# A third block of 128 output channels in the input-projection stage: the first LRU gate block accumulated while the modulation weights stream in

## The chip, the cores and the metric

The kernel runs on one core of one Trainium2 chip. The metric is the device time of one launch in microseconds; the kernel before takes 1186.78 us (median of three runs, 1185.78 to 1189.39). Matmuls run on TensorE (PE in the profile, its weight loads are PEld), elementwise work on VectorE (DVE), ScalarE (ACT) and GpSimd (POOL); SyncE (SP) issues most of the DMAs.

## The reference, cut to what matters

The block is one transformer layer on 1024 tokens of width 1024. What the change touches is its first third:

```python
mod = jnp.dot(jax.nn.silu(c), w_mod[l]) + b_mod[l]           # 1024 x 6144
shift1, scale1, gate1, shift2, scale2, gate2 = jnp.split(mod[:, None, :], 6, axis=-1)
h = rms_norm(x, g_norm1[l]) * (1.0 + scale1) + shift1
proj = jnp.dot(h, w_in[l])                                   # 1024 x 2560
x_lru, z_lru, q, k, v = jnp.split(proj, SPLITS, axis=-1)     # 512 channels each
...
y_lru = (h_fwd + h_bwd) * jax.nn.gelu(z_lru)
```

`x_lru` goes through a short convolution and two gated linear recurrences (the LRU); `z_lru` gates the result. Attention on q, k, v, an output projection and a mixture of 16 experts follow; the experts fill the time from about 615 us to the end.

## The kernel before, in words

Every float32 operand of a matmul is split in two float32r parts, high and low (`split`, L140: ACT copies the high part, another engine subtracts it to get the low part). A product is three matmuls: high by high, high by low, low by high. A block of 128 output channels over 1024 tokens and 1024 inputs (8 input tiles k = 0 to 7) takes 8 x 3 x 2 = 48 matmuls with 512 columns.

**The first stage** (L378 to L441) makes h and at once multiplies it with the first 256 columns of `w_in` (x_lru's channels 0 to 255, two blocks of 128, accumulated in the PSUM tiles `px[0]` and `px[1]`, named pjx). It goes input tile by input tile, since each tile of h needs its own 128 columns of shift and of scale, that is 1 MB of `w_mod`. The steps for one k are:

- `m_load(k)` (L282): four 256 KB DMAs on SP, `w_mod` into the tiles wm.
- `m_mm(k)` (L294): PE multiplies wm by silu(c) into the PSUM tile mp, for all 8 row blocks where k < 4 and for 4 of them (RP) where k >= 4.
- `m_sum(k)` (L301): DVE copies mp into acc; for k >= 4 it does the other 4 row blocks itself, four SCALAR_TENSOR_TENSOR of line L311, the first of which reads mp from PSUM and the other three only SBUF.
- `m_red(k)` (L315): four small matmuls of acc with ones, into pm: the sum over partitions.
- `m_col(k)` (L320): two small DVE operations make the column of 1 + scale and of shift.
- `h_make(k)` (L326): ACT makes the high part `hh`; ACT (k = 3 to 6) or DVE makes h in float32; POOL (k = 7: DVE) subtracts to get the low part `hl`, line L336.
- `x_mm(k, lo)` (L341): eight matmuls of pjx with hh (lo False) or four with hl (lo True).

In this stage PE, DVE and ACT run in the order in which the lines stand (`manual_schedule`, L378). For loop step k (L413 to L441) that is: `m_mm(k+2)`, `m_sum(k+2)`, the hh part of `x_mm(k)`, the hl part of `x_mm(k-1)`, `m_red(k+2)`, `m_col(k+2)`, `h_make(k+2)`. The weights' other half is split at step 1 (ACT) and step 3 (DVE, `w0_split(1,1)`), the small `lam_table` stands at step 4. SP and POOL are ordered by a scheduler, except that each DMA of the stage is tied behind the one before it (`issue_after(lds[-1])`).

**After it**, PE computes q and k (`proj_qk`, token tiles against 256 channels), the LRU of block 0 (`do_lru(0)`), more q and k, `do_lru(1)`, then the gate blocks z 0 and z 1 (`do_z`, L637: `proj_ch`, 48 matmuls into pjz; then `fin_lru`, Gelu on ACT and a product on DVE), with `mod_out(0)` (mq) between them, then the second half of x_lru, v, and so on. `mod_rest` (L619) adds up the remaining four sixths of the modulation on DVE (macc, L624) from 512 KB DMAs (wr). Weights come in 512 KB halves through five raw slots and six split slots (NRA, NSP). PSUM has two slots of tag pg and two of tag pj; px holds one of each during the first stage, pm used the other pg and mp the other pj.

Of the kernel before, what the change touches and what calls it, by code (L numbers as in the profile page):

```python
# [8 lines left out]
F32 = mybir.dt.float32  # L9
F32R = mybir.dt.float32r  # L10
# [3 lines left out]
ALU = mybir.AluOpType  # L14
# [48 lines left out]
KV = (7,)  # L63
KH = (0, 1, 2, 7)
KB = (0, 1, 2, 7)
CAP = 128
RPAD = 56
EPS = 1e-6
# [14 lines left out]
def tile_block(ctx: ExitStack, tc, x, cols, w_mod, b_mod, w_in, wa, wx, lam_qk, relT, w_out, g2, w_router,  # L83
# [8 lines left out]
    def mm(out, lhsT, rhs, start, stop):  # L92
        return T.matmul(out, lhsT=lhsT, rhs=rhs, start=start, stop=stop)  # L93
# [40 lines left out]
    def raw_tile(name, shape):  # L134
        return rawA.tile(shape, F32, tag="raw", bufs=NRA, name=name)
# [4 lines left out]
    def split(src, hi, lo, eng=None):  # L140
        act(hi, src)
        return (eng or V).tensor_tensor(out=lo, in0=src, in1=hi.bitcast(F32), op=ALU.subtract)  # L142

    def load_half(c0, kk, eng):
        r = raw_tile(f"wi{c0}_{kk}", [P, 4, 256])
        SY.dma_start(out=r, in_=w_in[kk * 512:(kk + 1) * 512, c0:c0 + 256].rearrange("(k p) c -> p k c", p=P))
        hi = strm.tile([P, 4, 256], F32R, tag="s", bufs=NSP, name=f"wi{c0}_{kk}h")
        lo = strm.tile([P, 4, 256], F32R, tag="s", bufs=NSP, name=f"wi{c0}_{kk}l")
        split(r, hi, lo, eng)
        return hi, lo  # L150

    def load_in(c0, eng):
        return [load_half(c0, kk, eng) for kk in range(2)]

    phb = ExitStack()
    psb = phb.enter_context(tc.tile_pool(name="psb", bufs=1, space=PSUM, reuse_waits="tile"))
# [125 lines left out]
    def m_load(k):  # L282
        for rh in range(2):
            w = raw_tile(f"wm{k}_{rh}", [P, 4, 2, P]) if rh else v_tile(f"wm{k}_{rh}", [P, 4, 2, P])
            for g in range(2):
                c0 = g * 1024 + k * P
                with tc.issue_after(lds[-1].ins):
                    lds.append(SY.dma_start(out=w[:, :, g, :],
                                            in_=w_mod[rh * 512:(rh + 1) * 512, c0:c0 + P].rearrange("(r p) c -> p r c", p=P)))
            wm[k, rh] = w  # L290
# [2 lines left out]

    def m_mm(k):  # L294
        if RP[k]:
            mps[k] = psb.tile([P, 2, P], F32, tag="pj", bufs=2, name=f"mp{k}")
        for r in range(RP[k]):
            g = 32 * (r % 4)
            mm(mps[k][g:g + 32], scz[:, r, :], wm[k, r // 4][:, r % 4], r < 4, r + 4 >= RP[k])
# [13 lines left out]
            V.tensor_tensor(out=part[0], in0=part[0], in1=part[1], op=ALU.add)  # L313

    def m_red(k):  # L315
        pms[k] = psb.tile([P, 2], F32, tag="pg", bufs=2, name=f"pm{k}")
        for g in range(2):
            mm(pms[k][:, g:g + 1], accs[k][:, g, :], ones32[:, 0:1], True, True)

    def m_col(k):  # L320
        pm = pms[k]
        V.scalar_tensor_tensor(out=acol[:, k:k + 1], in0=pm[:, 1:2], scalar=bs1[:, k:k + 1], in1=col[:, C_G1 + k:C_G1 + k + 1],
                               op0=ALU.add, op1=ALU.mult)
        V.tensor_tensor(out=shc[:, k:k + 1], in0=pm[:, 0:1], in1=col[:, C_BM + k:C_BM + k + 1], op=ALU.add)
# [16 lines left out]
    def x_mm(k, lo, ms=(0, 1)):  # L341
        for m in ms:
            wh, wl = (w[:, k % 4, m * P:(m + 1) * P] for w in ws0[k // 4])
            for lt, h_ in ((wh, hl[k]),) if lo else ((wh, hh[k]), (wl, hh[k])):
                for n in range(2):
                    mm(px[m][:, n * 512:(n + 1) * 512], lt, h_[:, n * 512:(n + 1) * 512],
                       k == 0 and lt is wh and not lo, k == KT - 1 and lo)

    w0r, wq0 = [], []

    def w0_load(kk):
# [18 lines left out]
    w0_load(0)  # L370
    for k in range(1, 4):
        m_load(k)
        if k == KM:
            w0_load(1)
    with tc.issue_after(lds[-1].ins):
# [2 lines left out]
    with tc.manual_schedule(engines={mybir.EngineType.PE, mybir.EngineType.DVE, mybir.EngineType.Activation}):  # L378
        c_silu()
        tables_a()  # L380
        act(rst[:, 0:1], epsc, AF.Sqrt)
        for t in range(NT + 1):
            if t < NT:
                x_stat(t)
            if 1 <= t <= NT:
                if t == NT:
                    m_mm(0)
                    m_sum(0)
                x_flip(t - 1)
                if t == NT:  # L390
                    m_red(0)
            if 2 <= t <= NT:
                x_evac(t - 2)
        w0_split(0, 0)
        m_col(0)
        x_evac(NT - 1, (0,))
        m_mm(1)
        warm(WU1)
        w0_split(0, 1)
        m_sum(1)  # L400
        h_make(0)
        m_red(1)
        m_col(1)
        x_evac(NT - 1, (1,))
        h_make(1)
        x_mm(0, False)
        m_mm(2)
        m_sum(2)
        x_mm(1, False, (0,))
        m_red(2)  # L410
        m_col(2)
        h_make(2)
        for k in range(1, KT + 1):  # L413
            if k + 3 < KT:
                m_load(k + 3)
            if k + 2 < KT:
                m_mm(k + 2)
                m_sum(k + 2)
            if k == KS:
                w0_split(1, 1)  # L420
            if k == 1:
                x_mm(0, True)
            if k == KLT:
                lam_table()
            if k < KT:
                x_mm(k, False, (0, 1) if k > 1 else (1,))
            if 1 < k < KT:
                x_mm(k - 1, True)
            if k + 2 < KT:
                m_red(k + 2)  # L430
                m_col(k + 2)
                i_act, i_pv = h_make(k + 2)
                if k + 2 < KT - 1:
                    i_pool = i_pv
                else:
                    i_dve = i_pv
            if k == KS0:
                w0_split(1, 0)
            if k + 2 in (KW, KW + 1):
                wq0.append(load_half(1024, k + 2 - KW, V))  # L440
        x_mm(KT - 1, True)  # L441
    sm1_.close()


# [51 lines left out]
    def do_lru(ct):  # L496
        xc = xc_[ct]
        xh = lt_(f"xch{ct}", None, F32R)
        xl = lt_(f"xcl{ct}", None, F32R)
        split(xc, xh, xl, V if ct in LV else G_)  # L500
        hs, st = [], []
        for d in range(2):
            pre = []
            for gi in range(2):
                pg = psb.tile([P, 1024], F32, tag="pg", bufs=2, name=f"pg{ct}_{d}_{gi}")
                i = d * 4 + ct
                for wi_, (w_, xv) in enumerate(((bdh, xh), (bdl, xh), (bdh, xl))):
                    for n in range(2):
                        mm(pg[:, n * 512:(n + 1) * 512], w_[gi][:, i, :], xv[:, n * 512:(n + 1) * 512], wi_ == 0, wi_ == 2)
                tg = lt_(f"tg{ct}_{d}_{gi}")  # L510
                act(tg, pg, AF.Tanh, scale=0.5, bias=hb[:, gi * 8 + i:gi * 8 + i + 1])
                pre.append(tg)
            ta, ti = pre
            i = d * 4 + ct
            tt = lt_(f"tt{ct}_{d}")
            act(tt, ta, AF.Tanh, scale=nkap[:, i:i + 1], bias=nkap[:, i:i + 1])
            act(ta, ta, AF.Exp, scale=kap[:, i:i + 1], bias=kap[:, i:i + 1])
            sq = lt_(f"sqa{ct}_{d}")
            act(sq, ta, AF.Square)
            V.scalar_tensor_tensor(out=tt, in0=sq, scalar=1.0, in1=tt, op0=ALU.add, op1=ALU.mult)  # L520
            V.scalar_tensor_tensor(out=ti, in0=ti, scalar=1.0, in1=xc, op0=ALU.add, op1=ALU.mult)
            st.append((ta, ti, tt))
        for d in range(2):
            ta, ti, tt = st[d]
            act(tt, tt, AF.Sqrt, scale=0.25)
            G_.tensor_tensor(out=ti, in0=ti, in1=tt, op=ALU.mult)
            if d == 0:
                V.tensor_tensor_scan(out=tt, data0=ta, data1=ti, initial=0.0, op0=ALU.mult, op1=ALU.add)
            else:
                V.tensor_tensor_scan(out=tt[:, ::-1], data0=ta[:, ::-1], data1=ti[:, ::-1], initial=0.0,  # L530
                                     op0=ALU.mult, op1=ALU.add)
            hs.append(tt)
        V.tensor_tensor(out=hs[0], in0=hs[0], in1=hs[1], op=ALU.add)
        hs_[ct] = hs[0]

    def fin_lru(ct, ps):
        ge = lt_(f"ge{ct}")
# [99 lines left out]
    def do_z(ws, cp, m):  # L637
        fin_lru(2 * cp + m, proj_ch(ws, m, f"pjz{cp}_{m}"))
# [3 lines left out]
    with tc.issue_after(conv.ins):  # L642
        mod_rest(0, 0, 1)
    do_lru(0)
    wq1 = load_in(1280, G_)
    mod_rest(0, 2)
    proj_qk(wk0, 1, 0)
# [3 lines left out]
    proj_qk(wq1, 0, 1)  # L651
    do_lru(1)
    mod_rest(0, 5)
    wz0 = load_in(512, G_)
    proj_qk(wk1, 1, 1)
    mod_rest(0, 6, 7)
    wx1 = load_in(256, V)
    do_z(wz0, 0, 0)
    pend.pop()[1]()
    mod_out(0)  # L660
    mod_new(1)
    do_z(wz0, 0, 1)
    mod_rest(1, 0, 1)
    wr = lru.tile([P, KT, NE], F32, name="wr")
    A.dma_start(out=wr, in_=w_router.rearrange("(k p) e -> p k e", p=P))
# [796 lines left out]
```

## Time and profile before

| | |
|---|---|
| median of 3 runs | 1186.78 us (1185.78 to 1189.39) |
| the profiled execution | 1189.59 us, its span 1187.8 us |
| PE / PEld busy | 94% / 79% of the span |
| DVE / ACT / POOL busy | 80% / 67% / 41% |
| mean granted TensorE clock | 0.979 |

The times of instructions are microseconds from the span's start. A busy share is an average over stages; how a stage is bound is read in its own stretch. An idle time in brackets stands at the instruction that ended it, with what released it.

### The profile page before, as it was taken

Reading aid. Unit: us, or ns where it says so; the run is one execution under the profiler, and the core shown is the slowest. Engines: PE = TensorE matmul, PEld = TensorE weight load, DVE = VectorE, ACT = ScalarE, POOL = GpSimd, SP = SyncE. Lnnn points to the kernel's source line nnn. Section 1 sums busy time; section 2 is a strip of 40 time slices with the busy share of each in tenths; the row PEclk is TensorE's granted clock in tenths of the full one; section 3 lists DMA queues with packets and bytes.
Section 4 is the critical chain, followed back from the end, with each engine's and each line's share of the span. In section 5 each row is a group of like instructions: output and inputs, shape, how many; then the busy total and the mean of one; then the engine's idle time right before and its main releaser. Section 6 shows DMA issues by size and latency. Waiting matters only on the chain.

```text
span 1187.8 us, 17864 instructions
## 1 busy us (share of the span) xinstructions
PE 1115.3 (94%) x6319; PEld 935.9 (79%) x6320; DVE 955.2 (80%) x1241; ACT 791.6 (67%) x1046; POOL 484.1 (41%) x540
## 2 busy tenths in 40 slices
PE   6999899999699999999649999999999999999996
PEld 4699898888588899777538788888888888888885
DVE  6797657874298897444579999999999999999995
ACT  7548282394177788544318788878887888888784
POOL 4693232133087547243544334443324444322400
PEclk9899999999899999999969999999999999999999
DMA  9765725723844604534799999999999999999911
GB/s 334 225 195 171 238 72 186 241 71 63 203 108 117 176 6 143 186 113 163 263 337 345 358 377 385 392 408 393 375 394 393 367 397 406 394 394 387 392 46 18
DMA packets 147889, 303.82 MB, mean 256 GB/s; under 512 B 17996, under 2 KB 44748, under 8 KB 147796
## 3 DMA queue, kind: packets, MB, share of 16 engines
q1 hardware_dynamic: 134864, 279.46, 65.9%
q0 software_dynamic: 5488, 19.45, 6.4%
q10 hardware_dynamic: 7448, 3.77, 1.1%
q8 instruction: 50, 0.82, 0.3%
q14 instruction: 39, 0.32, 0.1%
HBM read 277.42 MB, written 25.22 MB: 255 GB/s over the span
## 4 chain that ended last, share of the span: by engine, by line
PE 73%; DVE 7%; DMA 6%; POOL 6%; issue 5%; ACT 2%; SPq 0%; POOLq 0%; ACTq 0%; DVEq 0%
PE ab L93 28%; PE y L93 13%; PE mix L93 7%; PE pjk L93 3%; PE pjz L93 3%; PE pv L93 3%; PE sc L93 3%; POOL wo L886 2%; PE pjv L93 2%; DMA wr<-in_w_mod_dram 2%; PE pw L814 1%; PE pjx L93 1%; PE pf L1346 1%; PE pg L93 1%; DVE macc L624 1%
## 5 line engine op out<-in xcount | busy, mean ns | idle before, releaser
L1246 POOL TENSOR_SCALAR oh<-iot,slot 128x128 bf16<-128x128 bf16 x120 | 146.3, 1234 | 252.2 <-PE pf L1346 252.2
L93 PE MATMUL ab<-wh,xeh 128*128 128x512 f32 x512 | 202.0, 395 | 0.2 <-ACT xeh L90 0.2
L93 PE MATMUL ab<-wh,xel 128*128 128x512 f32 x512 | 199.7, 390 | 0.1
L93 PE MATMUL ab<-wl,xeh 128*128 128x512 f32 x512 | 157.7, 389 | 0.0
L93 PEld LDWEIGHTS ab<-wl,xeh 128*128 128x128 f32 x512 | 96.1, 188 | 20.3
L93 PEld LDWEIGHTS ab<-wh,xel 128*128 128x128 f32 x512 | 96.2, 188 | 19.4 <-DVE xel L1259 0.5
L93 PEld LDWEIGHTS ab<-wh,xeh 128*128 128x128 f32 x512 | 96.1, 188 | 19.4 <-ACT xeh L90 0.5
L142 DVE TENSOR_TENSOR wl<-w_0r,wh 128x1024 fp32r<-128x1024 f32 x79 | 96.8, 1226 | 10.2 <-ACT wh L90 0.4
L90 ACT ACTIVATE wh<-w_0r 128x1024 fp32r<-128x1024 f32 x81 | 86.0, 1062 | 24.9 <-PE ab L93 14.9
L142 DVE TENSOR_TENSOR wl<-w_3r,wh 128x1024 fp32r<-128x1024 f32 x79 | 96.6, 1224 | 6.2
L90 ACT ACTIVATE wh<-w_1r 128x1024 fp32r<-128x1024 f32 x79 | 83.5, 1058 | 23.6 <-PE ab L93 18.9
L90 ACT ACTIVATE wh<-w_3r 128x1024 fp32r<-128x1024 f32 x79 | 83.9, 1062 | 21.9 <-PE ab L93 18.2
L142 DVE TENSOR_TENSOR wl<-w_2r,wh 128x1024 fp32r<-128x1024 f32 x80 | 96.3, 1220 | 2.4 <-ACT wh L90 0.5
L90 ACT ACTIVATE wh<-w_2r 128x1024 fp32r<-128x1024 f32 x80 | 84.7, 1060 | 18.9 <-PE ab L93 17.9
L142 DVE TENSOR_TENSOR wl<-w_1r,wh 128x1024 fp32r<-128x1024 f32 x78 | 92.6, 1220 | 3.8 <-ACT wh L90 2.1
L768 DVE CUSTOM_DVE_ANT_0 p<-sc,bias 128x1024 f32<-128x1024 f32 x64 | 77.7, 1214 | 18.0 <-PE sc L93 18.0
L93 PE MATMUL y<-wh,htl 128*128 128x512 f32 x256 | 82.9, 395 | 0.0
L93 PE MATMUL y<-wh,hth 128*128 128x512 f32 x256 | 80.9, 396 | 0.0
L93 PE MATMUL y<-wl,hth 128*128 128x512 f32 x256 | 79.6, 391 | 0.0
L90 ACT ACTIVATE p<-p,stat 128x1024 f32<-128x1024 f32 x62 | 70.8, 1151 | 4.8 <-DVE stat L768 4.8
L93 PEld LDWEIGHTS pv<-v,wt 128*128 128x128 f32 x512 | 61.7, 192 | 2.4
L93 PE MATMUL pv<-v,wt 128*128 128x128 f32 x512 | 62.1, 275 | 0.0
(458 smaller groups left out, 2858.5 us busy)
## 6 DMA issues: line engine op xcount, KB each, us to landing
w_0r<-in_w_dram SPq DMA_DIRECT2D x81, 512.0 KB, 8.5
w_1r<-in_w_dram SPq DMA_DIRECT2D x79, 512.0 KB, 8.8
w_2r<-in_w_dram SPq DMA_DIRECT2D x78, 512.0 KB, 9.0
w_3r<-in_w_dram SPq DMA_DIRECT2D x77, 512.0 KB, 8.7
wr<-in_w_mod_dram SPq DMA_DIRECT2D x32, 512.0 KB, 4.7
wi<-in_w_in_dram SPq DMA_DIRECT2D x18, 512.0 KB, 4.7
w_5r<-in_w_dram SPq DMA_DIRECT2D x17, 512.0 KB, 6.8
wm<-in_w_mod_dram SPq DMA_DIRECT2D x32, 256.0 KB, 4.9
```

The lines of the kernel that those rows point to most:

```text
L90: return A.activation(out=out, in_=in_, func=func, **kw)
L93: return T.matmul(out, lhsT=lhsT, rhs=rhs, start=start, stop=stop)
L142: return (eng or V).tensor_tensor(out=lo, in0=src, in1=hi.bitcast(F32), op=ALU.subtract)
L624: V.scalar_tensor_tensor(out=macc[i], in0=w, scalar=sc[:, k:k + 1], in1=macc[i], op0=ALU.mult, op1=ALU.add)
L768: V.tensor_tensor_reduce(out=p_, in0=scp[g, j], in1=prs[h][0][:, b0:b0 + S], op0=ALU.add, op1=ALU.min, scale=1.0, scalar=3.0e38, accum_out ...
L814: T.transpose(pw[:, b * P:(b + 1) * P], pt_[g, 0][:, kt * P:(kt + 1) * P], ident)
L886: G_.tensor_tensor(out=r[:, qs], in0=r[:, qs], in1=gate1[:, qs], op=ALU.mult)
L1246: G_.tensor_scalar(out=oh[:, t, :], in0=iot, scalar1=slot[:, e, t:t + 1], scalar2=None, op0=ALU.is_equal)
L1346: T.transpose(pt[:, b * P:(b + 1) * P], sa[:, b * P:(b + 1) * P], ident)
```

## The change

z's first block (columns 512 to 639 of `w_in`) is moved into the first stage as a third block beside the two of x_lru. Its weights are one 512 KB DMA, issued between the modulation weights of k = 2 and of k = 3, into tiles of their own; they are split at step 1, the high part on ACT, the low part on DVE. `z_mm(k)` is six matmuls into the PSUM tile pz0, at the end of step k+1's PE work. In each step `m_red(k+2)` and `m_col(k+2)` now stand ahead of the hl part of `x_mm(k-1)`. Since pz0 takes the pg slot that pm used, pm for k > 2 lives in the second bank of mp's tile. The Gelu of z block 0 follows the stage at once, its product follows `do_lru(0)`. z's second block is loaded as one 512 KB column tile later on and stands alone where both stood.

```diff
+    def split_col(r, hi, lo, eng):
+        split(r, hi, lo, eng)
+        return [(hi[:, 4 * kk:4 * kk + 4, :], lo[:, 4 * kk:4 * kk + 4, :]) for kk in range(2)]
+
+    def load_col(c0, eng):
+        r = raw_tile(f"wc{c0}", [P, KT, P])
+        SY.dma_start(out=r, in_=w_in[:, c0:c0 + P].rearrange("(k p) c -> p k c", p=P))
...
     def m_mm(k):
         if RP[k]:
-            mps[k] = psb.tile([P, 2, P], F32, tag="pj", bufs=2, name=f"mp{k}")
+            mps[k] = psb.tile([P, 8, P], F32, tag="pj", bufs=2, name=f"mp{k}")[:, 0:5]
+            if k > 2:
+                pms[k] = mps[k].rearrange("p a b -> p (a b)")[:, 512:514]
+            mps[k] = mps[k][:, 0:2]
...
+    wz = [sm1.tile([P, KT, P], F32 if c == "r" else F32R, name=f"wz{c}") for c in "rhl"]
...
+    def z_load():
+        with tc.issue_after(lds[-1].ins):
+            lds.append(SY.dma_start(out=wz[0], in_=w_in[:, CZ:CZ + P].rearrange("(k p) c -> p k c", p=P)))
+
+    def z_split():
+        wzs[:] = split_col(*wz, V)
+
+    def z_mm(k):
+        if not pz:
+            pz.append(psb.tile([P, 1024], F32, tag="pg", bufs=2, name="pz0"))
+        wh, wl = (w[:, k % 4, :] for w in wzs[k // 4])
+        for lt, h_ in ((wh, hh[k]), (wh, hl[k]), (wl, hh[k])):
+            for n in range(2):
+                mm(pz[0][:, n * 512:(n + 1) * 512], lt, h_[:, n * 512:(n + 1) * 512], k == 0 and lt is wh and h_ is hh[k],
+                   k == KT - 1 and lt is wl)
...
     for k in range(1, 4):
         m_load(k)
+        if k == 2:
+            z_load()
...
                 x_mm(k, False, (0, 1) if k > 1 else (1,))
-            if 1 < k < KT:
-                x_mm(k - 1, True)
             if k + 2 < KT:
                 m_red(k + 2)
                 m_col(k + 2)
+            if 1 < k < KT:
+                x_mm(k - 1, True)
+            if k == KS0:
+                z_split()
+            if k < KT:
+                z_mm(k - 1)
+            if k + 2 < KT:
                 i_act, i_pv = h_make(k + 2)
...
         x_mm(KT - 1, True)
+        z_mm(KT - 1)
+        ge0 = ylp.tile([P, S], F32, tag="y", bufs=NCT, name="ylru0")
+        act(ge0, pz[0], AF.Gelu_apprx_tanh)
...
+    def fin_first():
+        V.tensor_tensor(out=ge0, in0=hs_[0], in1=ge0, op=ALU.mult)
+        y_lru.append(ge0)
...
     do_lru(0)
+    fin_first()
...
-    wz0 = load_in(512, G_)
+    wz0 = load_col(CZ + P, G_)
     proj_qk(wk1, 1, 1)
     mod_rest(0, 6, 7)
     wx1 = load_in(256, V)
-    do_z(wz0, 0, 0)
+    fin_lru(1, proj_ch(wz0, 0, "pjz0_1"))
     pend.pop()[1]()
     mod_out(0)
     mod_new(1)
-    do_z(wz0, 0, 1)
```

## Rows read from the trace of the kernel before

**Rows 1.** Stretches: length; PE, PEld, DVE, ACT, POOL busy; granted clock; DMA share; GB/s.

```profile
33.50:39.00 5.50, 2.89 (x12) 2.05 (x12) 5.37 (x4) 3.17 (x3) 4.55 (x2) 0.98 1.13 338
39.00:46.00 7.00, 6.95 (x25) 5.09 (x26) 5.04 (x7) 2.48 (x2) 2.41 (x1) 0.53 0.82 256
46.00:60.50 14.50, 14.50 (x81) 11.55 (x80) 11.19 (x23) 10.45 (x10) 10.17 (x13) 1.00 0.49 126
62.00:175.90 113.90, 108.45 (x855) 105.24 (x854) 83.50 (x64) 69.15 (x68) 50.07 (x39) 1.00 0.53 171
```

**Rows 2.** PE in order of time: start, us, instruction, idle before it and its releaser.

```profile
32.81 0.64 PE L93 MATMUL mp<-wm,scz 128*32 128x256 f32 x8
...
39.05 1.02 PE L93 MATMUL pm<-ones,acc 128*128 128x1 f32 x4 [2.66 <-DVE acc L311]
...
46.00 0.50 PE L93 MATMUL pm<-ones,acc 128*128 128x1 f32 x4
46.43 0.64 PE L93 MATMUL mp<-wm,scz 128*32 128x256 f32 x8
47.00 0.73 PE L93 MATMUL pjx<-hh,w0h 128*128 128x512 f32 x2
...
49.86 0.50 PE L93 MATMUL pm<-ones,acc 128*128 128x1 f32 x4
...
53.72 0.50 PE L93 MATMUL pm<-ones,acc 128*128 128x1 f32 x4
...
60.55 0.28 PE L93 MATMUL pjq<-wi_0h,hh 128*128 128x256 f32 x1
```

**Rows 3.** POOL in order of time, the same columns.

```profile
30.13 0.85 POOL L377 TENSOR_TENSOR lp<-lq 128x128 f32<-128x128 f32 x1 [2.46 <-DMA lq<-in_lam_qk_dram]
30.95 4.75 POOL L336 TENSOR_TENSOR hl<-h,hh 128x1024 fp32r<-128x1024 f32 x2
35.84 2.35 POOL L336 TENSOR_TENSOR hl<-xT,hh 128x1024 fp32r<-128x1024 f32 x1
43.02 2.41 POOL L336 TENSOR_TENSOR hl<-xT,hh 128x1024 fp32r<-128x1024 f32 x1 [4.83 <-ACT xT L90]
49.45 2.38 POOL L336 TENSOR_TENSOR hl<-xT,hh 128x1024 fp32r<-128x1024 f32 x1 [4.03 <-ACT xT L90]
```

**Rows 4.** The chain that ended last, pieces on DVE from 33.5 to 39 us.

```profile
33.52 0.49 DVE acc L311
...
34.03 1.96 DVE acc L311
...
36.02 2.46 DVE acc L311
...
38.51 0.50 DVE acc L311
```

**Rows 5.** DVE in order of time, the same columns as PE's.

```profile
43.10 3.40 DVE L363 TENSOR_TENSOR w0l<-w,w0h 128x1024 fp32r<-128x1024 f32 x1
46.54 0.22 DVE L322 SCALAR_TENSOR_TENSOR acol<-pm,bs,col 128x1 f32<-128x1 f32 x1
...
47.13 0.48 DVE L311 SCALAR_TENSOR_TENSOR acc<-wm,sc,mp 128x256 f32<-128x256 f32 x1 [0.32 <-PE mp L93]
47.65 1.53 DVE L311 SCALAR_TENSOR_TENSOR acc<-wm,sc,acc 128x256 f32<-128x256 f32 x3
...
57.60 1.22 DVE L142 TENSOR_TENSOR wi_0l<-wi,wi_0h 128x1024 fp32r<-128x1024 f32 x1
```

**Rows 6.** The chain that ended last, from 170 to 200 us.

```profile
175.94 10.91 PE pjz L93 x48
```

**Rows 7.** ACT in order of time, the same columns.

```profile
33.24 1.25 ACT L90 ACTIVATE hh<-xT,shc,acol 128x1024 fp32r<-128x1024 f32 x1 [2.15 <-DVE shc L324]
...
68.91 1.06 ACT L90 ACTIVATE bdh<-bd 128x1024 fp32r<-128x1024 f32 x1 [10.25 <-DMA bd<-in_wa_dram]
```

**Rows 8.** PE again, the one wait that follows z's two blocks within 50 us.

```profile
231.60 0.73 PE L93 MATMUL pg<-xch,bdh 128*128 128x512 f32 x2 [1.96 <-DVE lk L601]
```

More of the change, by code (lines that the diff above doesn't have):

```diff
@@ L65 @@
 KB = (0, 1, 2, 7)
+CZ = 512
 CAP = 128
@@ L153, in load_in @@
         return [load_half(c0, kk, eng) for kk in range(2)]
+    def split_col(r, hi, lo, eng):
[4 more added lines that the diff above has]
+        SY.dma_start(out=r, in_=w_in[:, c0:c0 + P].rearrange("(k p) c -> p k c", p=P))
+        return split_col(r, *(strm.tile([P, KT, P], F32R, tag="s", bufs=NSP, name=f"wc{c0}{c}") for c in "hl"), eng)
     phb = ExitStack()
@@ L315, in m_red @@
     def m_red(k):
-        pms[k] = psb.tile([P, 2], F32, tag="pg", bufs=2, name=f"pm{k}")
+        if k <= 2:
+            pms[k] = psb.tile([P, 2], F32, tag="pg", bufs=2, name=f"pm{k}")
         for g in range(2):
@@ L347, in x_mm @@
                        k == 0 and lt is wh and not lo, k == KT - 1 and lo)
+    wz = [sm1.tile([P, KT, P], F32 if c == "r" else F32R, name=f"wz{c}") for c in "rhl"]
+    wzs = []
+    def z_load():
[11 more added lines that the diff above has]
+                   k == KT - 1 and lt is wl)
+    pz = []
     w0r, wq0 = [], []
```

## Prediction, on record before the change was run

> **What bounds the kernel now.** I read the stretches first, then PE in order of time, then the engines that PE waits for. From 46 to 60.5 us PE is busy all the time, and from 62 to 175.9 us for all but 5.45 of 113.9 us [rows 1]; in the chain that ended last, z's block 0 stands with its 48 matmuls back to back, 10.91 us [rows 6]. So a matmul moved out of the late part saves its time there, and one put into the first stage costs its time, unless it falls into a hole. The first stage has one hole and one slow patch: PE sits idle 2.66 us before 39.05 us [rows 2], and from 39 to 46 us its granted clock averages 0.53, so it runs mostly at 1.2 instead of 2.4 GHz, right behind that idle time [rows 1]. That patch loses about 7.0 x 0.47 = 3.3 us.
>
> What makes the hole is the point to see. PE waits for acc on DVE. An acc step takes 0.48 to 0.5 us where it runs free, but two of those at 34 us take 1.96 and 2.46 us [rows 4, 5], and they end just after POOL's hl steps end: 30.95 + 4.75 = 35.70 against 34.03 + 1.96 = 35.99, and 35.84 + 2.35 = 38.19 against 36.02 + 2.46 = 38.48 [rows 3, 4]. The w0l split shows the same, 3.40 us beside POOL's hl at 43.02 us where such a split takes 1.22 us [rows 3, 5]. The step at 33.52 us that reads mp from PSUM takes 0.49 us although POOL is running [rows 3, 4]. So a DVE step with both inputs in SBUF stands still until the running POOL step is done, some 0.3 us past its end for an acc. The Trainium skill has this as a lock (SBUF — State Buffer, "Who interferes with whom"); the sum uses only the rows.
>
> From 46 us on the old order avoids this. Between two pm, 46.00 and 49.86 us, lie 3.86 us: pm 0.43, mp 0.57, then 12 matmuls in 2.86 us, 0.238 each with the gap [rows 2]. The acc steps follow mp at once (47.13 to 49.18 us), and POOL's hl comes after them (49.45 us) [rows 3, 5].
>
> **The change, part by part.**
>
> *Late part, removed.* 48 matmuls and their cover: -10.91 us [rows 6]. I take it in full, since PE is the bound there. What lay beside them (weight loads for x's second half, macc) loses 11 us of cover. The one PE wait that I see close behind is 1.96 us, for a DVE step [rows 8]; it may double or stay: 0 to +2, I take +0.5.
>
> *First stage, the load.* 512 KB more go ahead of k = 3's weights. At the 338 GB/s of that stretch [rows 1] this is 1.55 us by which all later loads land later, lq among them. POOL waited 2.46 us for lq [rows 3], and the hl of k = 1, 2 and 3 stand behind it on POOL, so they can all shift by up to 1.55 us.
>
> *The split.* Its ACT half (about 1 us) fits into the 2.15 us in which ACT waits before 33.24 us [rows 7]: nothing. Its DVE half reads only SBUF; it comes at about 33.3 us, stands until POOL's hl is done (33.33 to 34.9 us) and takes 1.22 us [rows 3, 5]. So the last two matmuls of z_mm(0) wait until 34.5 to 36.0 us, and mp of k = 4, at 32.81 us before [rows 2], starts 2 to 3.7 us later. Its three SBUF-only acc steps again meet two hl steps, now delayed themselves by the split. I get pm of k = 4 at 40.3 to 41.9 us instead of 39.05: +1.2 to +2.9, I take +2.0. The hole is not filled: pm now stands ahead of the hl matmuls of step k-1 and of z_mm, so PE waits with that work behind it.
>
> *The three steps from pm of k = 4 to pm of k = 7.* The new order on PE is pm, 4 hl matmuls, 6 of z, mp, 8 hh matmuls. If pm starts at 0: mp at 0.43 + 10 x 0.23 = 2.75; the first acc step, 0.70 after mp as at 47.13 [rows 2, 5], at 3.45 to 3.95. POOL's hl starts at 3.45, as 49.45 follows 46.00 [rows 2, 3], since ACT and DVE work behind pm is unchanged, and runs to 5.85. So the first SBUF acc ends at 6.15, the others at 6.65 and 7.2. PE has done its 8 matmuls at 5.25 and waits 1.95 us for the next pm. A step is 7.2 us instead of 3.86. Three are 21.6; the w0l split delays the second hl by another 0.5; a half clock behind these waits I put at +1.0 (0 to two patches of 3.3 us). Before, the same three steps took 53.72 - 39.05 = 14.67 us, the half-clock patch within [rows 2]. So +8.4 us.
>
> *The tail.* Behind pm of k = 7 stood 28 matmuls, 60.55 - 53.72 - 0.43 = 6.4 us [rows 2]; now there are 56 and no acc: +6.4 us.
>
> *Nothing, and what hides it.* Gelu and its table load at the stage's end: ACT sits idle 10.25 us before 68.91 us [rows 7]; the y product only changes its place on DVE. pm in mp's tile makes mp(k+1) wait for m_col(k), which starts 0.54 us after pm [rows 2, 5], while ten matmuls lie between. One y slot is held from the stage's end on, so the second macc memset on POOL may come late, 0 to +1 us; I take 0, as the tables ahead of it now start further ahead of PE. PE's 5.45 us of waits from 62 to 175.9 us [rows 1] belong to chains that shift with the stage: -1.5 to +1.5, I take 0.
>
> **The sum:** +2.0 + 8.4 + 6.4 = +16.8 us for the stage, -10.9 + 0.5 behind it: +6.4 us. The profiled execution took 1189.59 us (span 1187.8), 2.8 above the median of the runs shown; the difference goes on the median: 1186.8 + 6.4 = 1193.2 us. With the ends of the terms, this case spans about +2 to +12.
>
> **The rivals.**
>
> *The regimes interleave.* The stage has PE idle and DMA full, the late part the reverse, so moved matmuls fill the hole and the clock stays up: -2.66 - 3.3 = -6.0, 1180.8 us. The Trainium skill (Perfetto Trace Analysis, "Optimization Strategy") recommends such interleaving of regimes with different bounds; by that rule the sum would be this one. For it: the hole and the patch [rows 1, 2]. Against: the hole is made by POOL and DVE, and the order puts pm, which waits, ahead of the filler. It decides only if acc is ready when pm's turn comes.
>
> *The acc steps are not held up.* If they get through beside hl at 0.5 us each, a step is 0.43 + 2.3 + 0.57 + about 2.15 = 5.45, three are 16.4, +1.7; with pm of k = 4 unmoved and the tail +6.4 that is +8.1 - 10.9 = -2.8, 1184 us. Against it are all four held-up steps [rows 4, 5]; for it, that acc at 47.65 us ran free, so a small shift of phase decides: POOL's hl would have to start 2 us later.
>
> *The late gain is not cashed.* If 187 to 232 us turn out to be bound by DVE and the wr loads once z's cover is gone, half of the 10.9 us stays: +6.4 + 5 = +11.4, 1198 us. For it the wait of 1.96 us [rows 8]; against it PE's full stretches.
>
> That the matmuls don't move can't be: PE runs in written order there.
>
> **How the numbers follow.** A measurement of this kernel can tell about 0.3%, 3.6 us, from no change. The forecast case has 0.58 (0.06 of it within 3.6 us), the acc rival 0.20 (0.03 faster, 0.17 within), the interleaving 0.13 (faster), the lost late gain 0.09 (slower). Slower 0.61, same 0.23, faster 0.16. The range leaves out the interleaving and the extremes of the others: 1183.5 to 1200 us; the forecast case's own is 1189 to 1199.
>
> **What would show it.** Right: in the chain, acc steps of about 2.4 us beside every hl from k = 4 to 6; PE waits of about 2 us before the pm of k = 5, 6 and 7; pm to pm about 7 us; q's first matmul near 77 us instead of 60.55; one pjz block of 48 left near 190 us. Wrong: q's first matmul before 70 us, a granted clock near 1 from 39 to 46 us, or acc steps at 0.5 us beside hl.

## The result: slower by 1.3%, and the profile after

The changed kernel takes 1202.34 us (median of 4 runs, 1200.99 to 1203.98), the kernel before 1186.84 us beside it. The ratio is 1.0126, 95% interval 1.0100 to 1.0151. The forecast was 1193.2 us, at most 1200: the sign was right, the size was not. The profiled execution took 1203.98 us; its span is 1202.3 us, 14.5 more than before, at a mean clock of 0.971 instead of 0.979.

Four marks on PE, each the same work in both kernels, say where the 14.5 us lie:

| PE's mark | before | after | difference | forecast |
|---|---|---|---|---|
| q's first matmul (end of the stage) | 60.55 | 79.88 | +19.33 | +16.8 |
| from there to the last pjz block before mq | 115.39 | 118.95 | +3.56 | 0 |
| from there to ps2w, the router's product with shift2 | 88.99 | 82.20 | -6.79 | -10.4 |
| from there to attention's sc, as it stands in the chain | 46.77 | 45.19 | -1.58 | 0 |
| sum, at sc | 311.70 | 326.22 | +14.52 | +6.4 |

Behind sc nothing more is lost. So the stage missed by 2.5 us, 3.6 us were lost in the middle, which the forecast held to be free, and 3.6 us less than forecast came back from the late part; 1.6 us came back just ahead of sc, which the forecast did not have.

**The stage.** PE of the changed kernel in order of time, columns as in [rows 2]:

```profile
36.66 1.22 PE L94 MATMUL pz<-hh,wzl 128*128 128x512 f32 x2 [2.54 <-DVE wzl L143]
...
42.40 0.72 PE L94 MATMUL mp<-ones,acc 128*128 128x1 f32 x4
...
49.84 0.61 PE L94 MATMUL mp<-ones,acc 128*128 128x1 f32 x4 [1.64 <-DVE acc L324]
...
57.49 0.61 PE L94 MATMUL mp<-ones,acc 128*128 128x1 f32 x4 [2.02 <-DVE acc L324]
...
64.82 0.60 PE L94 MATMUL mp<-ones,acc 128*128 128x1 f32 x4 [1.68 <-DVE acc L324]
...
79.88 0.28 PE L94 MATMUL pjq<-wi_0h,hh 128*128 128x256 f32 x1
```

DVE and POOL of the same stage, the steps that share SBUF:

```profile
33.32 3.28 DVE L143 TENSOR_TENSOR wzl<-wzr,wzh 128x1024 fp32r<-128x1024 f32 x1
...
46.71 3.07 DVE L324 SCALAR_TENSOR_TENSOR acc<-wm,sc,acc 128x256 f32<-128x256 f32 x3
...
54.02 3.42 DVE L324 SCALAR_TENSOR_TENSOR acc<-wm,sc,acc 128x256 f32<-128x256 f32 x3
```

```profile
33.15 2.37 POOL L350 TENSOR_TENSOR hl<-h,hh 128x1024 fp32r<-128x1024 f32 x1
36.03 2.80 POOL L350 TENSOR_TENSOR hl<-xT,hh 128x1024 fp32r<-128x1024 f32 x1 [0.51 <-ACT xT L91]
46.07 2.39 POOL L350 TENSOR_TENSOR hl<-xT,hh 128x1024 fp32r<-128x1024 f32 x1 [7.24 <-ACT xT L91]
53.74 2.38 POOL L350 TENSOR_TENSOR hl<-xT,hh 128x1024 fp32r<-128x1024 f32 x1 [5.28 <-ACT xT L91]
```

The four mp rows from ones and acc are what [rows 2] calls pm: it lives in mp's tile now. From k = 4 to k = 7 they lie 7.44, 7.65 and 7.33 us apart, where the old kernel settled at 3.86. PE waits 1.6 to 2.0 us for acc before each of the last three. Three acc steps that take 1.53 us together where they run free [rows 5] take 3.07 to 3.42 us, since hl begins just before them; the first ends when hl does (in the chain, 54.02 + 2.39 = 56.41 against 53.74 + 2.38 = 56.12). The split of z's weights is held up in the same way, 3.28 us instead of 1.22.

The granted clock in three stretches (columns as in [rows 1]):

```profile
36.00:39.00 3.00, 2.34 (x11) 0.89 (x12) 0.64 (x2) 0.90 (x1) 2.80 (x1) 0.50 1.07 307
39.00:42.00 3.00, 3.00 (x8) 2.36 (x9) 1.89 (x4) 0.00 (x0) 0.00 (x0) 0.50 1.13 336
...
66.50:70.00 3.50, 3.50 (x10) 2.72 (x9) 3.04 (x4) 3.48 (x5) 3.16 (x5) 0.53 0.32 110
```

Behind the wait for wzl, and again behind the three waits for acc, PE runs at 1.2 GHz. The patch of [rows 1] from 39 to 46 us has moved, not gone.

**The middle.** The next lines are the stretch from q's first matmul to pjz and the one from there to ps2w, first of the kernel before:

```profile
60.55:175.94 115.39, 109.94 (x866) 106.72 (x865) 84.99 (x65) 69.18 (x69) 51.53 (x41) 1.00 0.54 173
175.94:264.93 88.99, 85.34 (x477) 72.96 (x476) 67.27 (x48) 42.86 (x42) 23.50 (x12) 1.00 0.52 166
```

and of the changed kernel:

```profile
79.88:198.83 118.95, 112.21 (x866) 109.03 (x865) 82.99 (x64) 70.40 (x69) 42.35 (x18) 0.97 0.48 157
198.83:281.03 82.20, 76.87 (x430) 66.08 (x429) 63.92 (x47) 40.90 (x40) 21.54 (x11) 0.96 0.56 173
```

In the middle PE has the same 866 matmuls. It is busy 2.27 us longer at a clock of 0.97, and idle 1.29 us longer (6.74 against 5.45). One wait stands out, 3.24 us longer than before while the others shrink: the transpose of k's norm, in the kernel before

```profile
128.00 1.09 PE L594 MATMUL pbk<-ident,nk 128*128 128x128 f32 x8 [1.18 <-DVE nk L587]
```

and in the changed one, with DVE's row of work ahead of it:

```profile
150.51 1.97 PE L642 MATMUL pbk<-ident,nk 128*128 128x128 f32 x8 [4.42 <-DVE nk L635]
```

```profile
144.05 1.27 DVE L672 SCALAR_TENSOR_TENSOR macc<-wr,sc,macc 128x1024 f32<-128x1024 f32 x1
145.25 1.21 DVE L581 TENSOR_TENSOR ylru<-tt,ylru 128x1024 f32<-128x1024 f32 x1
146.38 1.21 DVE L631 TENSOR_REDUCE rk<-sqk 128x16 f32<-128x1024 f32 x1
147.96 0.25 DVE L633 RECIPROCAL rk<-rk 128x16 f32<-128x16 f32 x1 [0.37 <-ACT rk L91]
148.13 1.19 DVE L672 SCALAR_TENSOR_TENSOR macc<-wr,sc,macc 128x1024 f32<-128x1024 f32 x1
149.24 1.22 DVE L635 TENSOR_TENSOR nk<-pjk,rk 128x1024 f32<-128x1024 f32 x1
```

Channel 0's product (ylru) and two steps of macc stand between the LRU and nk; in the kernel before none of the three did. By the starts of these rows they put nk off by 1.20 us (first macc), 1.13 us (the product) and about 0.9 us (second macc), together the 3.24 us. The transposes then take 1.97 us at half the clock.

**The late part.** One block of pjz is left in the chain, as long as in [rows 6], and 82.20 us behind its start comes ps2w:

```profile
198.83 10.91 PE pjz L94 x48
...
281.03 1.73 PE ps2w L94 x16
```

The wait of [rows 8] is still there, twice as long, and followed by half the clock (the two matmuls take 1.22 us instead of 0.73). By the windows above, the piece from pjz to ps2w has 1.7 us more idle time than before (5.33 against 3.65), and its matmuls take 2.4 us more than the old ones less z's 10.91 us, most of it (14.19 against 11.98 us) in the LRU's gate matmuls, pg, behind this wait:

```profile
246.06 1.22 PE L94 MATMUL pg<-xch,bdh 128*128 128x512 f32 x2 [4.16 <-DVE lk L649]
```

### The profile page after: what moved, and what is told of

It is laid out like the page before. It is cut to its first block, busy times and chain, and to the rows that moved or that the text cites. A ratio compares the mean times of both kernels' runs of the same rounds, so it can differ in the third digit from the quotient of the medians.

```text
span 1202.3 us, 17870 instructions
## 1 busy us (share of the span) xinstructions
PE 1123.6 (93%) x6320; PEld 940.6 (78%) x6320; DVE 952.2 (79%) x1242; ACT 793.1 (66%) x1047; POOL 482.7 (40%) x539
## 4 chain that ended last, share of the span: by engine, by line
PE 74%; DVE 8%; POOL 5%; DMA 4%; issue 4%; ACT 3%; SPq 0%; POOLq 0%; DVEq 0%; ACTq 0%
PE ab L94 27%; PE y L94 13%; PE mix L94 7%; PE pjk L94 3%; PE pjx L94 3%; PE pv L94 3%; PE sc L94 3%; PE pjz L94 2%; POOL wo L934 2%; PE pw L862 1%; PE pjq L94 1%; PE pf L1394 1%; DVE macc L672 1%; PE pg L94 1%; DMA wr<-in_w_mod_dram 1%
## 5 line engine op out<-in xcount | busy, mean ns | idle before, releaser
L94 PEld LDWEIGHTS ab<-wh,xeh 128*128 128x128 f32 x512 | 96.1, 188 | 19.3 <-ACT xeh L91 0.5
```

## The experiments

Theory: the order (pm ahead of the filler) together with z's ten matmuls between pm and mp puts the SBUF-only acc steps beside POOL's hl; that is the stage's excess over the 10.9 us of z itself. Beside it, two losses behind the stage from DVE work that changed its place. Rivals: the order alone does it, or z's matmuls cost their time wherever they stand; and late, the LRU instead of macc is the bound. Times between runs are compared by ratio to the kernel before on the same chip.

**The order alone, without z.** The kernel before, with m_red and m_col ahead of the hl part:

```diff
-            if 1 < k < KT:
-                x_mm(k - 1, True)
             if k + 2 < KT:
                 m_red(k + 2)
                 m_col(k + 2)
+            if 1 < k < KT:
+                x_mm(k - 1, True)
+            if k + 2 < KT:
                 i_act, i_pv = h_make(k + 2)
```

> The kernel before with the new order alone: m_red and m_col ahead of the hl part of x_mm, no z in the stage. Theory (POOL's hl steps hold up DVE's acc steps, and the new order brings them together): mp now starts 1.35 us after pm instead of 0.43, its last SBUF-only acc step meets hl at 3.45 us and ends near 6.4, so the three steps from pm of k = 4 to pm of k = 7 take about 19 us instead of 14.7, and 4 hl matmuls stand behind the first pm: +4 to +7 us, 1191 to 1194. Rival (the waits come from z's own matmuls and split, the order is harmless): within 1 us of before.

Measured: ratio 1.0032 (1.0003 to 1.0061); in the trace q's first matmul comes at 61.15 us, 0.6 later than before, and the pieces behind it are unchanged. The three steps from pm of k = 4 to pm of k = 7 take 15.51 us, not the expected 19; the ratio, with its wide interval, does not rule out the smaller end of the expected loss. For k = 5 acc does meet hl, and PE waits 2.10 us for it:

```profile
40.62 3.50 DVE L311 SCALAR_TENSOR_TENSOR acc<-wm,sc,acc 128x256 f32<-128x256 f32 x3
```

```profile
41.39 2.45 POOL L336 TENSOR_TENSOR hl<-xT,hh 128x1024 fp32r<-128x1024 f32 x1 [1.12 <-ACT xT L90]
```

In the next step acc runs ahead of hl:

```profile
46.97 1.53 DVE L311 SCALAR_TENSOR_TENSOR acc<-wm,sc,acc 128x256 f32<-128x256 f32 x3
```

```profile
48.08 2.64 POOL L336 TENSOR_TENSOR hl<-xT,hh 128x1024 fp32r<-128x1024 f32 x1 [4.25 <-ACT xT L90]
```

With four matmuls between pm and mp instead of ten, mp, and so acc, is early enough in two of the three steps. The order alone can make the collision, but not in every step, and the stage of this profile loses only 0.6 us.

**z early, in the old order.** The changed kernel, with m_red and m_col behind z_mm:

```diff
-            if k + 2 < KT:
-                m_red(k + 2)
-                m_col(k + 2)
             if 1 < k < KT:
                 x_mm(k - 1, True)
...
                 z_mm(k - 1)
             if k + 2 < KT:
+                m_red(k + 2)
+                m_col(k + 2)
                 i_act, i_pv = h_make(k + 2)
```

> The changed kernel with the old order: hl part of x_mm, then z_mm, then m_red and m_col. Theory: mp follows pm at once again, acc runs ahead of hl, a step is 0.43 + 0.57 + 18 x 0.23 = 5.15 us without a wait, the hole before pm of k = 4 is filled by z_mm; q's first matmul near 66 us instead of 79.9, 14 us less than the changed kernel: about 1188. Rival (what costs is z's work, its load and the half clock, not the order): 2 to 4 us less than the changed kernel, 1198 to 1200.

Measured: ratio 1.0027 (1.0009 to 1.0046), about 1% less than the changed kernel. q starts at 69.75 us. DVE and POOL of one step:

```profile
49.26 1.52 DVE L324 SCALAR_TENSOR_TENSOR acc<-wm,sc,acc 128x256 f32<-128x256 f32 x3
```

```profile
50.58 2.46 POOL L350 TENSOR_TENSOR hl<-xT,hh 128x1024 fp32r<-128x1024 f32 x1 [3.91 <-ACT xT L91]
```

Acc runs free, and PE waits for no acc step. The stage costs 9.2 us more than before, less than z's 10.9 us of matmuls, but q was expected near 66 us. So the order costs some 10 us of the 19.3 (6 to 10 us against the three profiles of the changed kernel's order below), but only with z in it: neither the order without z nor z without the order shows the collision in every step.

**No acc steps on DVE.** The changed kernel, all 8 row blocks of the modulation on PE:

```diff
-RP = (8, 8, 8, 8, 4, 4, 4, 4)
+RP = (8, 8, 8, 8, 8, 8, 8, 8)
```

> The changed kernel with all 8 row blocks of the modulation on PE for every k, so that DVE has no SBUF-only acc step left, only the copy out of PSUM. Theory: the waits before pm of k = 5, 6 and 7 (5.3 us in sum) go, a step is 0.43 + 2.3 + 1.0 + 1.84 = 5.6 us: 5 to 7 us less than the changed kernel, 1195 to 1197. Rival (pm waits for something else behind it, the loads or ACT): within 1 us of the changed kernel, or slower by the 24 added small matmuls.

Measured: ratio 1.0075 (1.0052 to 1.0098), q at 73.10 us. For acc DVE only copies, and PE has no wait before pm although the order is the new one:

```profile
46.17 0.42 DVE L318 COPY acc<-mp 128x256 f32<-128x256 f32 x1 [3.18 <-PE mp L94]
```

```profile
48.01 0.50 PE L94 MATMUL mp<-ones,acc 128*128 128x1 f32 x4
```

A step takes 5.83 us instead of 7.3 to 7.7, with more matmuls in it. The waits of the changed kernel are those of the three SBUF-only acc steps. The wait for wzl, 2.26 us, stays, as it should.

**The product late.** The kernel with the old order again, Gelu into a tile of the LRU's pool and channel 0's product behind z's second block:

```diff
-        ge0 = ylp.tile([P, S], F32, tag="y", bufs=NCT, name="ylru0")
-        act(ge0, pz[0], AF.Gelu_apprx_tanh)
...
+    ge0 = lt_("ge0")
+    act(ge0, pz[0], AF.Gelu_apprx_tanh)
...
     def fin_first():
-        V.tensor_tensor(out=ge0, in0=hs_[0], in1=ge0, op=ALU.mult)
-        y_lru.append(ge0)
+        y = ylp.tile([P, S], F32, tag="y", bufs=NCT, name="ylru0")
+        V.tensor_tensor(out=y, in0=hs_[0], in1=ge0, op=ALU.mult)
+        y_lru.insert(0, y)
...
-    fin_first()
...
     fin_lru(1, proj_ch(wz0, 0, "pjz0_1"))
+    fin_first()
```

> As the run with the old order, and beside it the Gelu of z block 0 in a tile of the LRU's pool, its product with the LRU only after z's second block, so that no y slot is held early and no product stands ahead of k's normalization on DVE. Theory (behind the stage the changed kernel loses 3.6 us between q and z, and about 2.5 behind z, to that DVE product and to the y slot that makes macc start late): 4 to 5 us less than the run with the old order, 1183 to 1184, below before. Rival (the lost cover is what counts there, not the place of the product): within 1 us of the run with the old order.

Measured: ratio 1.0004 (0.9987 to 1.0020), as fast as before. The stage is the same (q at 70.02); from there to pjz it takes 116.55 us where the run with the early product took 118.42. The transpose of k's norm waits 2.38 us instead of 4.44:

```profile
139.08 1.97 PE L642 MATMUL pbk<-ident,nk 128*128 128x128 f32 x8 [2.38 <-DVE nk L635]
```

The expected time below before did not come. The edit moves the product and also holds no y slot early; in DVE's order the product is gone from ahead of nk (1.13 us) and so is the second macc step (0.9 us), which together are the 2.06 us of the wait. So the early product, with the macc step that came with it, cost about 1.9 us. One macc step still stands ahead of nk and makes the wait 1.2 us longer than before; the next run shows whether that is what the remaining 1.2 us are.

**z between pm and the hl part.** On top of the last one:

```diff
-            if 1 < k < KT:
-                x_mm(k - 1, True)
...
                 m_col(k + 2)
+            if 1 < k < KT:
+                x_mm(k - 1, True)
+            if k + 2 < KT:
                 i_act, i_pv = h_make(k + 2)
```

> As the run with Gelu in the LRU's pool and the old order, but z_mm ahead of m_red and the hl part of x_mm behind it. There mp waited 0.4 to 1.0 us in each step for m_col, since pm now lives in mp's tile. Theory (those waits are that tile; four matmuls, 0.92 us, cover m_col, and four, unlike ten, still leave acc ahead of hl): a step takes 0.43 + 0.92 + 0.57 + 1.84 + 1.38 = 5.15 us, from pm of k = 2 to q's first matmul 37.5 us instead of 39.9, 2 to 3 us less in all. Rival (acc meets hl again as in the first step of the run with the order alone): steps of 6.2 us, no gain or up to 1 us more.

Measured: ratio 0.9996 (0.9978 to 1.0014), q at 70.54 us: no gain in the stage. Acc falls beside hl in the first two steps, and PE waits for it there:

```profile
40.90 0.61 PE L94 MATMUL mp<-ones,acc 128*128 128x1 f32 x4 [1.16 <-DVE acc L324]
47.28 0.61 PE L94 MATMUL mp<-ones,acc 128*128 128x1 f32 x4 [0.73 <-DVE acc L324]
```

The middle takes 115.14 us here, as long as before, although the transpose of k's norm waits as long as in the last run. The clock does not fall behind the wait:

```profile
139.61 1.09 PE L643 MATMUL pbk<-ident,nk 128*128 128x128 f32 x8 [2.37 <-DVE nk L636]
```

So the 1.2 us that the run before this one still lost in the middle are the half clock behind that wait (its matmuls there are busy 111.37 us, here 109.97), not the wait itself.

**The late macc steps moved away.** On top of the late product, the second half's steps of macc all go behind the projection of v that carries do_lru(2):

```diff
-    mod_rest(1, 0, 1)
...
-    mod_rest(1, 2, 3)
...
-    mod_rest(1, 5, 6)
+    mod_rest(1, 0, 1, 2, 3, 5, 6)
```

> As the run with Gelu in the LRU's pool and the old order, but the macc steps of input tiles 0 to 3 of the second modulation half (8 DVE steps and their 512 KB loads) come after the third LRU block instead of ahead of it. Theory (with z's cover gone, DVE's macc steps and their loads hold up what PE waits for behind z): from the first pjz matmul to shift_logits' first 79 us or less instead of 81.9, 2 to 4 us less in all. Rival (the chain of conv, split and LRU itself is what PE waits for): within 1 us.

> Both edits together on top of the run with Gelu in the LRU's pool. Theory: the gains add, 4 to 6 us less than that run and 0.3 to 0.5% less than the kernel before. Rival (chains behind take it back): within 0.1% of the kernel before.

> The kernel before with the same macc steps moved behind the third LRU block, no z in the stage. Theory (it is the lost cover that makes these steps matter): at most the 1.96 us wait goes, 0 to 2 us less than before. Rival (the steps cost the same without z in the stage): 3 us less or more.

The second of these has both this edit and z between pm and the hl part, the third has this edit alone in the kernel before. Measured: ratios 0.9990 (0.9971 to 1.0010), 1.0003 (0.9983 to 1.0022) and 1.0027 (1.0006 to 1.0048). PE's waits of the first, from 195 to 272 us (total, times, longest):

```profile
PE pg L94 <- ACT tg L91: 4.7, 1, 4.7
PE pg L94 <- DVE lk L649: 0.3, 1, 0.3
```

The wait for lk is gone, and one for ACT's tg, of the same LRU, has come in its place. From pjz to ps2w it takes 82.12 us where it took 81.86 with the macc steps. So macc does hold lk up, but taking it away gives nothing back. In the second run the same distance is 81.25 us, with a wait of 4.4 us for tg. None of the three theories held. In the first two runs the time stays level, as their rivals have it. In the third, the kernel before, neither came: the edit leaves the wait for lk at 1.97 us, and the piece from the last pjz block before mq to ps2w takes 91.39 us instead of 88.99. The late product alone had already cut the wait for lk to 1.48 us, with the full clock behind it, but there the wait for tg is 2.84 us and the clock falls behind that one (0.61 from 261 to 264 us). Its piece of 81.86 us holds five pjz matmuls more than the changed kernel's, about 1.2 us, so it is some 1.5 us better and no more. The two waits of this LRU add up to 4.3 to 5.6 us in every version with one z block, and to 3.65 us before.

**The product's line moved alone, and the changed kernel again.** In the changed kernel:

```diff
     do_lru(0)
-    fin_first()
...
     wx1 = load_in(256, V)
+    fin_first()
     fin_lru(1, proj_ch(wz0, 0, "pjz0_1"))
```

> The changed kernel, with one line moved: channel 0's product with the early gate (VectorE, 1.21 us) is no longer issued right behind channel 0's LRU but where the kernel before had it, behind the second projection of the gate. From q's first matmul to the gate's second projection the changed kernel takes 118.95 us, the kernel before 115.39. If it is the product, ahead of k's norm on VectorE, that makes the transpose of k wait 4.4 instead of 1.2 us and lets the clock fall, this distance comes back to 115.5 to 117 and the ratio to before falls by 0.2 to 0.3% against the changed kernel (to about 1.010). Rival: the two steps of macc on VectorE, not the product, are what k's norm stands behind; then the distance stays at 118 to 119 and the wait at 3 to 4.4 us. The stage before q (79.9 us) and the stage behind the gate (82.2 us) stay in both.

> The changed kernel itself, on the same chip as the run with the late product, so that the two can be compared: ratio to before 1.0126 as measured at first (1.010 to 1.015), gate's second projection 118 to 120 us behind q's first matmul.

Measured: 1.0109 (1.0091 to 1.0128) and 1.0104 (1.0085 to 1.0123). The line stands just ahead of the gate's second projection, not behind it as the expectation says. The first run decides nothing about the product: behind the stage a scheduler orders DVE, and it put the product at the same place, 1.2 us behind the start of a macc step, so that DVE's order of work is that of the changed kernel. Its use is as a repeat. The three profiles of this order have q's first matmul at 79.88, 78.21 and 76.10 us, then 118.95, 119.00 and 118.98 us to pjz, and 82.20, 81.96 and 81.89 to ps2w. The two losses behind the stage are steady, the stage is not: in the fastest of the three the split of z's weights slipped past hl,

```profile
33.43 1.22 DVE L143 TENSOR_TENSOR wzl<-wzr,wzh 128x1024 fp32r<-128x1024 f32 x1
```

and PE waited for it 0.47 us instead of 2.54.

## Why the prediction was wrong in size

**The mechanism in the stage was right.** PE's waits before pm, the acc steps beside each hl and the pm distances came as written in the profiled run and in one of its repeats, and the runs with the old order and without acc steps show that order and acc steps together make them. In the fastest repeat (q at 76.10 us) the distances are the same, 7.31, 7.66 and 7.32 us, but partly for another reason: only one of the three steps has its wait (2.00 us), and in the other two matmuls at half the clock fill the time. Its sum of +16.8 us lies between the three profiles (+15.6, +17.7, +19.3). By term: pm of k = 4 was put at 40.3 to 41.9 us and came at 42.40, 40.88 and 40.26; the three steps were put at 23.1 us and took 22.4, 22.3 and 22.3; the tail was put at about 13.2 us with pm and took 15.1, 15.1 and 13.6, the longest with the half-clock patch at 66.5 us that the forecast had placed among the steps. In the profiled run this is 2.5 us of the miss.

**The first step that failed** is "the y product only changes its place on DVE: nothing", with "-1.5 to +1.5, I take 0" for the middle. The middle cost +3.6 us in all three profiles. The waits there do belong to chains, but one chain got new links: the product moved ahead of k's norm, and the scheduler also let macc steps through ahead of it, so the transposes waited 4.42 us instead of 1.18. The run with the late product gives back 1.9 us, and the one with z between pm and hl all of it: with a wait of 2.37 us and no fall of the clock behind it the middle is as long as before. So the step failed by two terms, new work ahead of nk and the half clock behind the longer wait. Why the macc steps moved as they did was not tested.

**The second** is the late term, -10.9 with "0 to +2, I take +0.5" for lost cover. It gave back 6.8 to 7.1 us in the three profiles, so the loss of cover cost about 4, not 0.5. The row for it stood there [rows 8], and its growth to 4.2 us is near the double that the bound allowed; what was left out is the clock, 2.4 us of longer matmuls beside 1.7 us of more idle time. In the kernel before DVE did eight macc steps (191.77 to 209.2 us) under z's second block and what follows, ahead of x's first column step at 210.79 us. In the changed one no z block follows mq, both memsets of macc come at 212.83 us, right behind a split on POOL, and macc's first four steps begin at 218.50 us:

```profile
218.50 5.12 DVE L672 SCALAR_TENSOR_TENSOR macc<-wr,sc,macc 128x1024 f32<-128x1024 f32 x4 [2.68 <-DMA macc<-in_b_mod_dram]
```

The others then stand between x's steps and lk. The y slot that is held early is not the reason: in the run with the late product, which holds none, the memsets also come 2.3 us behind mq's start. "The late gain is not cashed" was the nearest rival, with half of z's time lost and a chance of 0.09; its size was nearly right, and its cause half: with macc out of the way, or the wait for lk short, the LRU's tg on ACT takes over. What would shorten that chain was not tried, so what bounds the piece from pjz to ps2w in all versions with one z block stays open.

**The other rivals.** Interleaving did not come: in the changed kernel the hole was neither filled nor removed. The Trainium skill's advice (Perfetto Trace Analysis, "Optimization Strategy"), that interleaving stretches with different bounds may improve the time, is not borne out by this case: even in the four runs with the late product it comes out level, with ratios of 0.9990 to 1.0004, whose intervals all hold 1. The rival "acc steps not held up" fails for the kernel as changed, but its mechanism is what the old order gives; its time, 1184 us, is not, since the losses behind the stage stay. That a DVE step with two inputs in SBUF and a POOL step shut each other out is as the Trainium skill states it (SBUF — State Buffer, "Who interferes with whom"), and the rows agree: 1.5 us for three steps alone, 3.1 to 3.4 beside hl, and hl itself 3.39 us instead of 2.37 in the repeat where the split began 0.09 us ahead of it.

No version beat the kernel before. The best ones, z early with a late product, are level with it: z's matmuls cost 8.5 to 10 us in the stage and 0 to 1 in the middle, and give back 6.5 to 8 later, in some of them 2 more ahead of sc.

## What to carry to other kernels

Put filler ahead of the instruction that waits, and work out what each of its matmuls does to the phase of the engines behind it: with four matmuls between pm and mp acc met hl in one or two steps, with ten in nearly every one. When a block of matmuls is taken out of a full stretch, list what the elementwise engines did under it; its time comes back only as far as they have room elsewhere. A new idle time of PE is priced together with the slower matmuls that may follow it, in every stage and not only where the old trace shows them.

## What the hardware showed that was not expected

- The slower clock cost more than the waits in the middle: 2.27 us of longer matmuls against 1.29 us of more idle time, with eight transposes in 1.97 us against 1.09 before.
- A wait alone does not tell whether the clock falls. Behind 1.18 us and behind 1.96 us [rows 8] it stayed at 1.00; behind 2.38, 4.16 and 4.42 us it went to 0.50; behind 2.37 us, at the same place in another run, it stayed at 1.00; from 46 to 66.5 us of the changed kernel it stayed at 1.00, with waits of 1.64, 2.02 and 1.68 us in it, and fell only then.
- One POOL step of 2.4 us and one DVE step decide by tenths of a microsecond who goes first: the same split took 1.22, 2.67 and 3.28 us in three profiles of the same order, and the stage's end moved by 3.8 us with it and what followed.
